# Five mixed chunks of the RWKV receptance kept as parts in DRAM for the second half of the columns

## The chip, the cores and the metric

The kernel runs on one core of one Trainium2 chip. The metric is the time of one execution in device microseconds, as the median of several runs. The core has a matrix engine (TensorE, here PE, with its weight loads shown as PEld), a vector engine (VectorE, DVE), an activation engine (ScalarE, ACT), a general engine (GpSimd, POOL) and a queue engine (SyncE, SP) that issues nearly all DMA transfers of this kernel.

## The reference, cut to what matters

The program is a two-layer causal decoder trunk of 512 positions and 1024 channels in float32. The second layer's mixer is RWKV-7 time mixing. What the change touches is the receptance r:

```
xx = jnp.pad(h, ((0, 0), (1, 0), (0, 0)))[:, :-1] - h
xr, xw, xk, xv, xa, xg = [h + xx * mix[i] for i in range(6)]
r = (xr @ w_r).astype(f32)
...
_, y = lax.scan(rwkv7_step, jnp.zeros((B, H, N, N), f32), seqs)
```

So r is a product of a mixed input (each position blended with the one before it, by one factor per channel) with a 1024 x 1024 matrix. k and v are made in the same way, with other factors. r then enters the recurrence over the positions.

## The kernel before

Channels lie on the partitions, in eight chunks c0 to c7 of 128 channels, with the 512 positions along the free axis. To keep float32 accuracy each operand of a large product is split into two parts, a high part (a cast to the matrix engine's format) and a low part (the value less its high part), and each product is made as three matmuls: high by high, high by low, low by high (`mm3`).

The three projections of RWKV are written by `project`, each in two halves of 512 output columns. A half takes the eight chunks one after the other, with four output banks: for each of c0 to c5 it makes 4 x 3 matmuls, and at its end c6 and c7 are done bank by bank, so that the banks can be evacuated (`evac_r` and others). The weights come as parts from DRAM, where an earlier stage parked them (`L288`), one 512 KB transfer for each chunk and half, into four places that are used in turn.

The mixed chunk that a half needs is made by `mixed`: ACT scales h into a row (`L1361`), DVE adds the scaled neighbour (`L1363`, the blend), ACT casts the row to the high part (`L1372`), and DVE or POOL subtracts for the low part (`L1374`; for r it is DVE for c0 and POOL for the others). For k and v the eight pairs of parts are kept in SBUF for the second half. For r there is no room, and `mixed` is called again in the second half. Here h0 and h1 are the first and the second half of the columns of r, at about 1498 to 1534 us and 1534 to 1575 us of the profiled span.

The counter `n` in `mixed` goes on through all calls: 17 to 24 in h0 of r, 25 to 32 in h1. Where `n % 3` is not 0 the parts of a chunk go to one of two places in `parts_all` (place 0 if `n % 3` is 1, place 1 if it is 2), otherwise to a buffer of the ring `xm`. In h0 these are place 1 for c0, c3 and c6, place 0 for c2 and c5, and xm for c1, c4 and c7; in h1 place 0 for c0, c3 and c6, place 1 for c1, c4 and c7, and xm for c2 and c5.

Beside the halves of r other work is woven in by steps (`weave`): the decay of the second group of heads (`rw_decay`, two products into the banks rq, two evacuations by ACT at `L102`, a running sum on DVE at `L1535` and two exponentials at `L102`), its keys (`rw_keys`), the inverse of the first group (`rw_inverse`, 62 small DVE steps at `L1641` and `L1647`, a 1024-wide ACT copy at `L1656`, writes to and reads from DRAM, and small products), and after h1 the ties and the recurrence, into which the second inverse is woven. The order on PE is pinned as written; the order on the other engines comes from a scheduler that works with modelled times. SP issues its transfers in one order, and a transfer that must wait holds up all behind it.

Of the kernel before, what the change touches and what calls it, by code (L numbers as in the profile page):

```python
# [11 lines left out]
F32 = mybir.dt.float32  # L12
F32R = mybir.dt.float32r
# [6 lines left out]
P = 128  # L20
D = 1024
S = 512
# [27 lines left out]
class Trunk:  # L50
# [1287 lines left out]
    def rwkv(self, gain):  # L1338
        nc, mm = self.nc, self.nc.tensor.matmul
# [12 lines left out]
            )  # L1352

        self.mid = None
        n_mix = [0]

        def mixed(i, c, dep=None):

            n = n_mix[0] = n_mix[0] + 1
            t = self.row("mx", 3) if i == 2 else self.rows[:, n % 2, :]  # L1360
            ins = nc.scalar.activation(t, h[c], AF.Copy, scale=v["mix1"][:, i, c : c + 1])  # L1361
            self.after(ins, dep)
            nc.vector.scalar_tensor_tensor(  # L1363
                out=t[:, 1:], in0=h[c][:, : S - 1], scalar=v["mix"][:, i, c : c + 1], in1=t[:, 1:],
                op0=ALU.mult, op1=ALU.add,
            )
            if i == 0 and n % 3:

                m = self.shaped(self.parts_all[:, (n % 3 - 1) * 2 * S : n % 3 * 2 * S], [2, S])
            else:  # L1370
                m = self.pair("xm", 9, F32R)
            nc.scalar.copy(m[:, 0, :], t)  # L1372
            eng = nc.vector if i == 2 or i == 0 and c == 0 else nc.gpsimd
            eng.tensor_tensor(out=m[:, 1, :], in0=t, in1=m[:, 0, :].bitcast(F32), op=ALU.subtract)  # L1374
            return m[:, 0, :], m[:, 1, :]

        k_t = [None] * NCH
# [28 lines left out]
        def project(half, xm, evac, natural, i_mix=None):  # L1406
# [11 lines left out]
            for k in range(NCH):  # L1418
                if k % 2 == 0:
                    w += self.next_w()  # L1420
                if half == 0 or xm is None:
                    if i_mix == 2:
                        normed(k)
                    xs[k] = mixed(i_mix, k, dep)
                if k < 6:
                    for b in range(4):
                        tile(k, b)
                    if k == 4:
                        self.mid = self.last_mm
                    if k == 5 and i_mix == 2:  # L1430
                        self.after(self.rwkv_tables(), self.last_mm)
                    yield
# [18 lines left out]
        xm = {}  # L1451
# [8 lines left out]
        xm = {}  # L1460
# [507 lines left out]
```

## Time and profile before

| | |
|---|---|
| median of 3 runs | 2130.84 us (2129.04 to 2134.41) |
| the profiled execution's own time | 2133.98 us |
| its span | 2132.3 us |
| mean granted PE clock | 0.985 of full speed |
| PE busy | 2049.5 us, 96% of the span |
| DVE, ACT, POOL busy | 74%, 45%, 6% |
| DMA | 282.42 MB, 132 GB/s over the span |

The profile shows one execution. A row names the line of the kernel, the engine, the operation, and the tiles that it writes and reads. The idle time in brackets is what the engine stood still just before a row, with what ended it. Times within the span are microseconds from its start.

### The profile page before, as it was taken

The numbers are of one execution on the slowest core, as the hardware profiler recorded it, in microseconds if no ns is written. First come the engines' busy times: TensorE is split into PE (matmuls) and PEld (weight loads), VectorE is DVE, ScalarE is ACT, GpSimd is POOL, SyncE is SP. The second block draws the span as 40 slices with busy tenths as digits, with TensorE's granted clock in tenths as the row PEclk, the third lists the DMA queues.
The fourth block names the chain that finished last, engine by engine and source line by source line (L and its number), as shares of the span: only waits on it lengthen the run. The fifth ranks groups of instructions, "written<-read, shape, count | busy, mean of one in ns | idle before, by whom it ended". The sixth has DMA issues, their size and how long they took to land.

```text
span 2132.3 us, 29206 instructions
## 1 busy us (share of the span) xinstructions
PE 2049.5 (96%) x11527; PEld 1642.7 (77%) x11527; DVE 1580.0 (74%) x1985; ACT 960.5 (45%) x1389; POOL 124.1 (6%) x165
## 2 busy tenths in 40 slices
PE   8999999999989999999999999999888999999998
PEld 6788888776877788888878787876666668888887
DVE  7778786467667988797788888556976547887784
ACT  5433444354455544445544444373634425433342
POOL 0000000211000000000000000112332100000000
PEclk9999999999999999999999999999989999999999
DMA  5333332421132567763355664536644232333321
GB/s 169 89 118 101 98 99 72 124 79 51 45 104 62 172 221 240 238 208 127 99 194 187 214 207 158 207 129 207 200 118 107 84 117 86 105 103 119 109 89 40
DMA packets 219297, 282.42 MB, mean 132 GB/s; under 512 B 45395, under 2 KB 135659, under 8 KB 219160
## 3 DMA queue, kind: packets, MB, share of 16 engines
q1 hardware_dynamic: 216520, 278.20, 41.4%
q10 hardware_dynamic: 2640, 2.36, 0.3%
q8 instruction: 91, 1.49, 0.3%
q14 instruction: 46, 0.38, 0.1%
HBM read 227.76 MB, written 54.59 MB: 132 GB/s over the span
## 4 chain that ended last, share of the span: by engine, by line
PE 76%; DVE 12%; DMA 5%; ACT 3%; issue 2%; SPq 1%; POOL 0%; DVEq 0%; ACTq 0%; POOLq 0%
PE fp L120 36%; PE fd L120 17%; PE am L120 6%; PE rm L120 4%; DVE parts L297 2%; PE rq L120 2%; PE wo L120 2%; PE rr L120 2%; PE rl L120 1%; DVE const L1641 1%; DMA wx<-in_rw_wk_dram 1%; DVE const L1647 1%; PE fd L691 1%; ACT parts L296 1%; DVE const L293 1%
## 5 line engine op out<-in xcount | busy, mean ns | idle before, releaser
L120 PE MATMUL fp<-parts,xs 128*128 128x512 f32 x2016 | 493.6, 393 | 11.7 <-DVE parts L297 6.4
L120 PEld LDWEIGHTS fp<-parts,xs 128*128 128x128 f32 x2016 | 378.4, 189 | 95.0 <-DVE parts L297 9.5
L120 PE MATMUL fd<-act,parts 128*128 128x512 f32 x1728 | 409.2, 390 | 2.2 <-DVE acts L332 1.6
L296 ACT CAST parts<-wx 128x1024 fp32r<-128x1024 f32 x224 | 233.9, 1052 | 354.6 <-PE fp L120 167.4
L120 PEld LDWEIGHTS fd<-act,parts 128*128 128x128 f32 x1728 | 323.7, 188 | 72.3 <-DVE acts L332 3.4
L297 DVE TENSOR_TENSOR parts<-wx,parts 128x1024 fp32r<-128x1024 f32 x224 | 272.1, 1220 | 71.3 <-ACT parts L296 71.1
L296 ACT CAST parts<-const 128x1024 fp32r<-128x1024 f32 (+1 forms) x192 | 198.2, 1033 | 267.4 <-PE fp L120 137.0
L120 PE MATMUL fp<-parts,xb 128*128 128x512 f32 x1152 | 291.5, 400 | 6.6 <-ACT wx L668 3.3
L297 DVE TENSOR_TENSOR parts<-const,parts 128x1024 fp32r<-128x1024 f32 (+1 forms) x192 | 230.2, 1200 | 58.1 <-ACT parts L296 57.1
L120 PEld LDWEIGHTS fp<-parts,xb 128*128 128x128 f32 x1152 | 216.2, 191 | 53.5 <-ACT wx L668 3.9
L654 DVE TENSOR_TENSOR wx<-fp,wx 128x1024 f32<-128x1024 f32 x140 | 168.8, 1219 | 24.0 <-PE fp L120 23.8
L712 DVE SCALAR_TENSOR_TENSOR const<-fd,const 128x512 f32<-128x512 f32 x160 | 108.9, 686 | 82.5 <-PE fd L120 82.1
L120 PE MATMUL fp<-parts,xa 128*128 128x512 f32 x576 | 144.6, 400 | 3.0 <-ACT xa L572 2.0
L120 PEld LDWEIGHTS fp<-parts,xa 128*128 128x128 f32 x576 | 110.2, 193 | 27.6 <-ACT xa L572 2.6
L120 PE MATMUL am<-xg,parts 128*128 128x512 f32 x384 | 100.0, 411 | 0.0
L416 POOL TENSOR_TENSOR ssum<-ssum,sq 128x512 f32<-128x512 f32 x14 | 22.9, 1639 | 1180.1 <-ACT sq L415 1179.7
L120 PEld LDWEIGHTS am<-xg,parts 128*128 128x128 f32 x384 | 71.8, 191 | 25.4 <-issue 9.4
L102 ACT ACTIVATE wx<-wx,const 128x512 f32<-128x512 f32 x80 | 53.5, 716 | 47.0 <-DVE wx L654 46.9
L242 ACT CAST acts<-wx 128x1024 fp32r<-128x1024 f32 (+2 forms) x37 | 37.1, 1003 | 53.8 <-DMA wx<-in_rw_wv_dram 14.4
L331 ACT CAST act<-fd 128x512 fp32r<-128x512 f32 x80 | 43.7, 588 | 38.2 <-PE fd L691 38.0
L120 PE MATMUL rm<-xm,parts 128*128 128x512 f32 x252 | 60.8, 394 | 0.0
L243 DVE TENSOR_TENSOR acts<-wx,acts 128x1024 fp32r<-128x1024 f32 (+2 forms) x37 | 43.0, 1163 | 23.8 <-ACT acts L242 23.7
(319 smaller groups left out, 2637.8 us busy)
## 6 DMA issues: line engine op xcount, KB each, us to landing
wx<-in_ffn_w_down_dram SPq DMA_DIRECT2D x72, 512.0 KB
parts<-acts SPq DMA_DIRECT2D x68, 512.0 KB
parts<-parts SPq DMA_DIRECT2D x68, 512.0 KB
wx<-in_ffn_w_gate_dram SPq DMA_DIRECT2D x44, 512.0 KB
wx<-in_ffn_w_up_dram SPq DMA_DIRECT2D x40, 512.0 KB
const<-in_ffn_w_up_dram SPq DMA_DIRECT2D x40, 512.0 KB
const<-in_ffn_w_gate_dram SPq DMA_DIRECT2D x36, 512.0 KB
const<-in_ffn_w_down_dram SPq DMA_DIRECT2D x16, 512.0 KB
```

The source lines that it names most:

```text
L102: ins = nc.scalar.activation(out, in_, func, **kw)
L120: return self.pe(self.nc.tensor.matmul(*args, **kw))
L242: nc.scalar.copy(hi, src)
L243: nc.vector.tensor_tensor(out=lo, in0=src, in1=hi.bitcast(F32), op=ALU.subtract)
L293: self.nc.vector.tensor_tensor(out=out, in0=in0, in1=in1, op=ALU.add)
L296: self.last_cast = self.nc.scalar.copy(hi[:r, :n], raw[:, :n])
L297: self.nc.vector.tensor_tensor(out=lo[:r, :n], in0=raw[:, :n], in1=hi[:r, :n].bitcast(F32), op=ALU.subtract)
L331: self.nc.scalar.copy(hi, t)
L416: nc.gpsimd.tensor_tensor(out=ssum, in0=ssum, in1=sq, op=ALU.add)
L654: add = lambda out, other, ps=ps: nc.vector.tensor_tensor(out=out, in0=ps, in1=other, op=ALU.add)
L691: nc.tensor.transpose(ps[:, b * P : (b + 1) * P], us[n][b][:, f * P : (f + 1) * P], self.ident)
L712: nc.vector.scalar_tensor_tensor(out=self.x[c], in0=ps, scalar=0.5, in1=self.x[c], op0=ALU.mult, op1=ALU.add)
```

## The change

The condition and the placing of the parts are moved into `room`. A chunk of r whose parts went to `parts_all` is stored to a DRAM tile of 512 KB (both parts) right after it is made. Where `mixed` is asked for a chunk that has such a tile, it makes nothing, and loads the parts from DRAM into the place or ring buffer that is its turn. In h0 c0, c2, c3, c5 and c6 are stored, and in h1 they are loaded. The condition of the store stands for both halves.

```diff
-        n_mix = [0]
+        n_mix, kept = [0], {}
...
+            def room():
+                if i == 0 and n % 3:
+
+                    return self.shaped(self.parts_all[:, (n % 3 - 1) * 2 * S : n % 3 * 2 * S], [2, S])
+                return self.pair("xm", 9, F32R)
+
+            if i == 0 and c in kept:
+
+                m = room()
+                self.after(nc.sync.dma_start(m.bitcast(F32), kept[c]), dep)
+                return m[:, 0, :], m[:, 1, :]
             t = self.row("mx", 3) if i == 2 else self.rows[:, n % 2, :]
...
-            if i == 0 and n % 3:
-
-                m = self.shaped(self.parts_all[:, (n % 3 - 1) * 2 * S : n % 3 * 2 * S], [2, S])
-            else:
-                m = self.pair("xm", 9, F32R)
+            m = room()
             nc.scalar.copy(m[:, 0, :], t)
             eng = nc.vector if i == 2 or i == 0 and c == 0 else nc.gpsimd
             eng.tensor_tensor(out=m[:, 1, :], in0=t, in1=m[:, 0, :].bitcast(F32), op=ALU.subtract)
+            if i == 0 and n % 3:
+                kept[c] = self.dram.tile([P, 2, S], F32, name=f"mix{c}")
+                nc.sync.dma_start(kept[c], m.bitcast(F32))
```

The lines below the change stand 11 further down in the changed kernel (`L1600` becomes `L1611`). The order of the instructions on PE stays the same. On ACT, around the change from h0 to h1, the kernel before has from the inverse's 1024-wide copy on (r_10494 to r_10496 are the evacuations r1 to r3 of h0's banks, L1555 a step of the keys, the two L102 rows the exponentials of the fourth decay, the CAST to parts that of c1):

```order
L1656 COPY const_66<-const_66 128x1024
L1600 COPY r_10494<-rm_10280 128x512
L1555 ACTIVATE heads_10336<-pa_10338,const_66 128x512
L1600 COPY r_10495<-rm_10281 128x512
L1372 CAST xm_10584<-const_66 128x512
L1372 CAST parts_67<-const_66 128x512
L1600 COPY r_10496<-rm_10282 128x512
L1562 ACTIVATE heads_10336<-heads_10336 128x8
L102 ACTIVATE heads_10336<-heads_10336 128x512
L102 ACTIVATE us_10337<-heads_10336 128x512
L98 ACT_TABLE_LOAD
```

In the changed kernel ACT has at the same place, from the evacuation r0 (r_10503) on, with r1 to r3 as r_10504 to r_10506:

```order
L1611 COPY r_10503<-rm_10279 128x512
L1667 COPY const_66<-const_66 128x1024
L1566 ACTIVATE heads_10340<-pa_10342,const_66 128x512
L102 ACTIVATE heads_10340<-heads_10340 128x512
L102 ACTIVATE us_10341<-heads_10340 128x512
L98 ACT_TABLE_LOAD
L1380 CAST parts_67<-const_66 128x512
L1611 COPY r_10504<-rm_10280 128x512
L1573 ACTIVATE heads_10340<-heads_10340 128x8
L1611 COPY r_10505<-rm_10281 128x512
L1566 ACTIVATE heads_10340<-pa_10342,const_66 128x512
L1611 COPY r_10506<-rm_10282 128x512
```

The evacuations r1 to r3 moved behind the exponentials, the table load and c1's cast; c2's cast is gone.

On SP the kernel before has, for the time in which h1 begins (parts362 to parts368 are the weights of h1, two chunks each, parts372 weights of a later step, tout0 and uout0 the tiles through which the inverse goes to DRAM and back):

```order
L288 DMA parts_67<-parts372_8060 96x1024
L1655 DMA tout0_10128<-const_66 128x1024
L288 DMA parts_67<-parts364_7674 128x1024
L1662 DMA const_66<-tout0_10128 32x32x32 x2
L288 DMA parts_67<-parts364_7674 128x1024
L1657 DMA uout0_10129<-const_66 128x1024
L288 DMA parts_67<-parts366_7771 128x1024
L1672 DMA us_9526<-uout0_10129 32x32x32 x3
L288 DMA parts_67<-parts366_7771 128x1024
L1672 DMA us_9526<-uout0_10129 32x32x32
L288 DMA parts_67<-parts368_7864 128x1024 x2
```

In the changed kernel the same stretch of SP is (mix1 and mix4 as destinations are stores of c1 and c4 of h1, mix3 as a source the load of c3):

```order
L288 DMA parts_67<-parts372_8060 96x1024
L1666 DMA tout0_10128<-const_66 128x1024
L1668 DMA uout0_10129<-const_66 128x1024
L288 DMA parts_67<-parts364_7674 128x1024 x2
L1673 DMA const_66<-tout0_10128 32x32x32 x2
L1683 DMA us_9526<-uout0_10129 32x32x32
L1385 DMA mix1_10564<-parts_67 128x1024
L1683 DMA us_9526<-uout0_10129 32x32x32 x3
L1370 DMA parts_67<-mix3_10362 128x1024
L288 DMA parts_67<-parts366_7771 128x1024 x2
L1385 DMA mix4_10694<-parts_67 128x1024
L288 DMA parts_67<-parts368_7864 128x1024
```

The store of c1 now stands before three of the four reads of uout0, the load of c3 behind them, and the weights of c4 and c5 (parts366) behind that load.

## Rows read from the trace of the kernel before

**Rows 1.** The page's busy time of PE and its share of the span:

```profile
PE 2049.5 (96%) x11527; PEld 1642.7 (77%) x11527; DVE 1580.0 (74%) x1985; ACT 960.5 (45%) x1389; POOL 124.1 (6%) x165
```

**Rows 2.** Busy time of each engine in stretches of the span (start:end, length, then for each engine its busy us and the number of instructions, the granted PE clock, the share of the DMA engines in use, GB/s):

```profile
1484.00:1488.00 4.00, 4.00 (x18) 3.02 (x18) 0.50 (x3) 0.00 (x0) 0.00 (x0) 1.00 1.02 400
...
1500.00:1512.00 12.00, 11.00 (x48) 7.83 (x46) 11.66 (x20) 4.00 (x10) 6.03 (x6) 1.00 1.02 339
1512.00:1524.00 12.00, 8.06 (x28) 5.45 (x29) 11.52 (x20) 8.78 (x16) 4.29 (x4) 0.80 0.30 103
...
1536.00:1548.00 12.00, 10.19 (x97) 6.78 (x96) 12.00 (x16) 6.61 (x13) 4.00 (x3) 1.00 1.04 257
1548.00:1560.00 12.00, 9.11 (x86) 6.83 (x87) 11.94 (x18) 4.93 (x10) 3.89 (x3) 0.72 0.27 85
```

**Rows 3.** What PE's matmuls waited for in 1498 to 1576 us (us in total, times, longest):

```profile
PE rq L120 <- ACT us L102: 4.2, 2, 3.5
PE rm L120 <- ACT parts L1372: 2.2, 1, 2.2
PE rm L120 <- POOL parts L1374: 2.0, 2, 1.3
...
PE rm L120 <- ACT r L1600: 0.6, 1, 0.6
```

**Rows 4.** PE's timeline (start, us, what, number of matmuls, in brackets the idle time before and what ended it). The row at 1480.28 is in the second half of v; 1520.26 and 1521.84 are in h0, the others in h1:

```profile
1480.28 6.20 PE L120 MATMUL rm<-parts,xm 128*128 128x512 f32 x25 [1.75 <-DMA parts<-parts]
...
1520.26 1.64 PE L120 MATMUL rq<-hids,parts 64*128 64x512 f32 x5 [3.45 <-ACT us L102]
1521.84 5.00 PE L120 MATMUL rm<-parts 128*128 128x512 f32 x12
...
1534.41 2.65 PE L120 MATMUL rm<-parts 128*128 128x512 f32 x9
...
1540.08 2.79 PE L120 MATMUL rm<-parts 128*128 128x512 f32 x11 [0.65 <-POOL parts L1374]
...
1543.22 3.06 PE L120 MATMUL rm<-xm,parts 128*128 128x512 f32 x12
...
1549.56 0.50 PE L120 MATMUL rm<-parts 128*128 128x512 f32 x1 [2.15 <-ACT parts L1372]
1551.40 5.06 PE L120 MATMUL rm<-parts 128*128 128x512 f32 x11 [1.33 <-POOL parts L1374]
...
1557.68 3.04 PE L120 MATMUL rm<-parts 128*128 128x512 f32 x12
```

**Rows 5.** The chain of waits in order of time (start, us, what): the transfer that begins the first inverse, c0's subtraction, the last step of the inverse, c3's blend (DVE counts there from the end of the step before), the subtractions of c4 and c3, PE's last group of h1, and the transfer that begins the second inverse:

```profile
1480.69 6.61 DMA const<-lin
...
1529.57 0.60 DVE parts L1374
...
1531.11 0.19 DVE const L1647
...
1546.89 0.67 DVE const L1363
...
1548.41 2.95 POOL parts L1374 x2
...
1572.11 2.96 PE rm L120 x12
...
1585.20 3.70 DMA const<-lin
```

**Rows 6.** ACT's timeline around the start of h1: the inverse's copy, r1, a key step, r2, c1's cast, r3, the two exponentials, the table load, and the first step of a chunk behind it:

```profile
1532.23 2.13 ACT L1656 COPY const<-const 128x1024 f32<-128x1024 f32 x1
1534.23 0.61 ACT L1600 COPY r<-rm 128x512 f32<-128x512 f32 x1
1534.71 0.85 ACT L1555 ACTIVATE heads<-pa,const 128x512 f32<-128x512 f32 x1
1535.43 0.60 ACT L1600 COPY r<-rm 128x512 f32<-128x512 f32 x1
...
1536.42 0.65 ACT L1372 CAST parts<-const 128x512 fp32r<-128x512 f32 x1
1536.94 0.62 ACT L1600 COPY r<-rm 128x512 f32<-128x512 f32 x1
...
1537.53 0.66 ACT L102 ACTIVATE heads<-heads 128x512 f32<-128x512 f32 x1
1538.05 0.66 ACT L102 ACTIVATE us<-heads 128x512 f32<-128x512 f32 x1
1538.73 1.28 ACT L98 ACT_TABLE_LOAD   x1
1540.02 0.72 ACT L1361 ACTIVATE const<-const 128x512 f32<-128x512 f32 x1
```

**Rows 7.** Timelines of POOL and DVE: a subtraction on POOL, and two steps of the inverse on DVE, one within the POOL row's time and one behind it:

```profile
1493.49 1.62 POOL L1374 TENSOR_TENSOR parts<-const,parts 128x512 fp32r<-128x512 f32 x1 [1.84 <-ACT parts L1372]
...
1493.88 1.41 DVE L1641 TENSOR_TENSOR const<-const 128x156 f32<-128x156 f32 x1
...
1495.68 0.34 DVE L1641 TENSOR_TENSOR const<-const 128x175 f32<-128x175 f32 x1
```

**Rows 8.** SP's timeline: the issue of the first three reads of uout0:

```profile
1542.27 1.53 SPq L1672 DMA_DIRECT2D us<-uout  x3
```

## The prediction

> **What bounds the kernel now.** I read the page's busy shares first: the reader sees TensorE (PE) busy for 96% of the span [rows 1], so nearly everything that a change can win or lose shows as time in which PE stands still or is granted its lower clock. Then the stretches around the change, 1484 to 1560 us, in a table of windows [rows 2]: the clock column is 1.00 except in 1512 to 1524 (0.80) and 1548 to 1560 (0.72), and PE's busy time falls short there and in 1536 to 1548. DVE is full in all rows from 1500 to 1560, and the DMA column says 1.02 in 1500 to 1512, 0.30 after it, and 1.04 in 1536 to 1548.
>
> Next, PE's own waits in these 78 us [rows 3]: 4.2 us for ACT's evacuations of the decay products, 2.2 us for ACT and 2.0 for POOL on the mixed chunks, 0.6 for the evacuation of r. PE's timeline [rows 4] puts them in order. In the first half (h0) PE stands for 3.45 us before the row at 1520.26, and the 12 products behind it take 5.00 us, where 12 take 3.04 in the row at 1557.68. In the second half (h1), whose c0 begins at 1534.41, PE waits 0.6 us for r [rows 3], 0.65 (POOL, c1), 2.15 (ACT, c3) and 1.33 (POOL, c3) [rows 4], and the 11 products of c3 take 5.06 us, against 2.79 for 11 of c1. From 1551.40 on PE does not wait in h1.
>
> Last, the chain of waits [rows 5] shows what is late there: DVE works without a break from the end of the inverse at 1531.30 to 1546.89, where c3's blending step comes up at last; ACT's cast and two POOL subtractions follow, and at 1551.40 PE takes over up to its last product of h1, which starts at 1572.11 in a group of 12. ACT's evacuation, the lin transfers and the second inverse hang on that, so what h1 wins or loses goes through to the end one for one: the recurrence starts from it, and the feed-forward layer behind is PE's own time.
>
> **Removed.** For c0, c2, c3, c5 and c6 of h1 two ACT steps, one DVE blend and one subtraction go (DVE's for c0, POOL's for the rest): 0.72 + 0.65 us of ACT, 0.67 of DVE as the chain counts a blend, and about 1.5 of POOL each (two in 2.95) [rows 5, 6]. None of that counts by itself, since PE is the bound; what counts is that c3 no longer waits behind DVE's queue. Its two waits go, 2.15 + 1.33 us, and so does the low clock behind them, 5.06 - 2.79 = 2.27: together 5.75 us. c4 keeps its own steps, but its blend stands some 20 rows earlier on DVE, inside the inverse, so it isn't late: its cast waits for c1's products only.
>
> **Added on SP.** The condition for a store is the same in both halves, so there are eight stores, not five: c1, c4 and c7 of h1 are written to DRAM too, and nothing loads them. With the five loads that is 13 transfers of 512 KB, 6.8 MB more. A transfer of that size took 3.70 us in a quiet stretch and 6.61 in a full one [rows 5]. c2's and c5's loads go to buffers of their own, long ahead. c0's waits for the last reader of its place, c5 of h0, whose products end by 1526.8 (1521.84 + 5.00) [rows 4]; with 3.70 to 6.61 it lands by 1533.4 at the latest, and PE wants it at 1534. I cost these three at nothing. c3's load stands behind c1's store and the four reads of the inverse, and its place is free when c0 is done, at 1540.1 by the working below: issued at about 1540.9, it lands between 1544.6 and 1547.5, or at 1548.8 with a further 512 KB before it (1.3 us at the 400 GB/s of 1484 to 1488) [rows 2]. PE asks for c3 at 1548.1. So nothing, with 2.0 us as the upper end, if three neighbours and not one come before it. Behind c1's store wait the reads of the inverse: the store waits for POOL's subtraction of c1, some 1.5 us after a cast at 1536.3, so it goes out near 1538.6, and the reads are issued by 1540.5, where in before the first began at 1542.27 [rows 8]. Nothing lost. c6's load waits for c3's products and has some 10 us until PE wants it.
>
> **Moved on ACT.** This is the part that the diff doesn't tell. In before ACT evacuates r1 right behind the 1024-wide copy; now r1, r2 and r3 stand behind that copy, a key step, the two exponentials of the fourth decay, the table load and c1's cast. By the distances of starts [rows 6]: copy 2.00, key step 0.72, exponentials 0.52 and 0.68, table load 1.29, cast 0.52, r1 0.61, together 6.34 us. The copy waits for the inverse, which DVE ended at 1531.30 and now ends 1.3 us sooner (c0's blend 0.67 and subtraction 0.60 gone) [rows 5], at 1530.0; ACT has r0 and one more step ahead of it. I let the copy start at 1531.1, half way between 1530.0 and the 1532.23 of before. Then r1 ends at 1537.4, r2 at 1538.0, r3 at 1539.3, and c0's second group of products waits for r1 from about 1534.8 on, some 2.6 to 3.4 us. c0 ends at 1540.1, the spread product takes 0.4, and c1's 12 products run from 1540.5 to 1543.5, where in before they ended at 1542.8 (the row at 1543.22 less 0.4) [rows 4]: +0.7 us, between -0.4 and +1.8 with the two ends for the copy.
>
> The Trainium skill (ScalarE: Activation LUTs, What ACT_TABLE_LOAD costs) gives a switch of tables 1.28 us for the load and about 1.38 for a drain beside it. The row has 1.28 and the next step starts 0.01 us behind it [rows 6], so this trace shows no drain; by the page r1 would end 1.4 us later and the sum below be -1.8.
>
> **The clock.** A wait of about 3 us lies before c0's second group. In before the stands of 3.45 and of 2.15 + 1.33 us were each followed by the low clock (0.80 and 0.72 over their windows, one of the two levels, 1.2 of 2.4 GHz), at a price of 5.00 - 3.04 = 1.96 and of 2.27 us; the one of 1.75 us at 1480.28 was not: 25 products in 6.20, 0.25 each [rows 2, 4]. I expect the low clock on c1 and c2, at +1.8 (a little under 1.96, since part of it falls on products that wait for r2 and r3 anyway), between 0 and 2.27.
>
> **Sum.** -5.75 + 0.7 + 1.8 = -3.2 us, between -5.75 - 0.4 = -6.2 and -5.75 + 1.8 + 2.27 + 2.0 = +0.3. The profiled execution took 2133.98 us (span 2132.3); it would be 2130.8. The median of before is 2130.84, 3.1 us below that execution; the same 3.2 off it gives 2127.6.
>
> **Rivals.**
> *DVE sets the end (faster).* POOL and DVE hinder each other here: an inverse step of 156 columns took 1.41 us beside a POOL subtraction, one of 175 columns 0.34 alone [rows 7]. Four subtractions fewer give DVE 4 x 1.07, five blends 3.35, c0's subtraction 0.6: 8.2 us. If all of h1 follows DVE, as the chain does up to 1546.89, the time is 2130.84 - 8.2 = 2122.6. Against it: PE's queue is closed from 1551.40 on, and r1 on ACT comes before it. The Trainium skill (GPSIMD Engine Reference, Specifications) says that the two engines share an SBUF interface and contend when DVE reads two SBUF inputs; the rows above agree.
> *The wait only moves (no change).* c3's load lands at 1551 instead of 1548, PE stands about as long as before and the low clock follows it: the 5.75 come back, 2130.8 or up to 1 us on either side. For it: DMA is at 1.04 in 1536 to 1548 [rows 2], and c1's store and c3's load fall into it. Against it: the second load of the c4/c5 weights is pushed behind them.
> *Stores starve h0 (slower).* The stores of c0, c2, c3, c5 and c6 stand on SP before the weight loads of h0, in a stretch with DMA at 1.02 [rows 2], and one waits there for POOL. Each is 1.3 us of transfer; if PE comes to wait for all five, 6.5 us, and for the low clock once, 2.0, the sum is -3.2 + 8.5 = +5.3: 2136.1. It decides once the weights' lead is under 1.3 us. For it: PE waited 1.75 us for weights at 1480.28 [rows 4]. Against it: no such wait leads PE's list after 1498 [rows 3], the DMA column of 1512 to 1524 says 0.30 [rows 2], and one issue of weights per finished chunk leaves a lead of three chunks.
>
> **Chances.** The forecast 0.60, DVE sets the end 0.15, the wait only moves 0.15, stores starve h0 0.10. The three runs of before lie from 2129.04 to 2134.41, and about 0.3% (6.4 us) is what a measurement here can tell from no change: below 2124.4 is faster, above 2137.2 slower. Faster holds most of the first rival and the low edge of the forecast, 0.18; slower half of the last and some of what I haven't thought of, 0.10; the rest, 0.72, is within. The range of 8 in 10 goes from 2121.5 to 2134.5: the sum's ends from the median, 2124.7 and 2131.1, widened by some 3 us on either side for the spread of the runs and the two nearer rivals.
>
> **What would show it.** Right: PE waits about 3 us for ACT r behind c0's first group; no wait for c3, or for DMA, in h1; the low clock on c1 and c2 and not on c3; PE's last group of h1 some 3 us earlier. If PE doesn't wait for r1, the ACT term is wrong; if it waits for a DMA before c3 or c6, the load term; if it waits for weights in h0, the last rival holds. A time under 2122 or over 2135 says that something outside h1 moved.

## The result and the profile after

The changed kernel took 2140.09 us (median of 9 runs, 2135.74 to 2142.79), the kernel before 2134.23 us in the same comparison (9 runs, 2129.04 to 2137.57). The ratio is 1.0027, with a 95% interval from 1.0017 to 1.0036: slower by about 5.9 us, where 3.2 us of gain were forecast, and outside the range.

PE is as full as before [rows 1], at a mean granted clock of 0.982 against 0.985. The page's busy line of the changed kernel:

```profile
PE 2051.9 (96%) x11527; PEld 1647.8 (77%) x11527; DVE 1575.0 (74%) x1979; ACT 953.9 (45%) x1379; POOL 118.2 (6%) x161
```

What PE's matmuls waited for in the halves of r and somewhat beyond, 1498 to 1578 us, which answers to [rows 3]:

```profile
PE rq L120 <- ACT us L102: 3.9, 1, 3.9
PE rm L120 <- ACT r L1611: 2.5, 1, 2.5
PE rm L120 <- DMA parts<-mix: 0.7, 1, 0.7
```

The waits for c1's and c3's parts are gone, and a wait for r has grown from 0.6 to 2.5 us. PE's timeline of h1, which answers to [rows 4], with its first group, c3 and the last group:

```profile
1538.02 0.98 PE L120 MATMUL rm<-parts 128*128 128x512 f32 x3
1541.54 2.74 PE L120 MATMUL rm<-parts 128*128 128x512 f32 x9 [2.54 <-ACT r L1611]
...
1552.88 3.01 PE L120 MATMUL rm<-parts 128*128 128x512 f32 x12 [0.73 <-DMA parts<-mix]
...
1571.28 3.02 PE L120 MATMUL rm<-parts 128*128 128x512 f32 x12
```

The last group of h1 in before:

```profile
1572.04 3.02 PE L120 MATMUL rm<-parts 128*128 128x512 f32 x12
```

h1 begins at 1538.02 and ends at 1571.28 + 3.02 = 1574.30: 36.28 us. In before it took from 1534.41 [rows 4] to 1572.04 + 3.02 = 1575.06: 40.65 us. So h1 gained 4.4 us. ACT's timeline shows why PE waits at its start, as against [rows 6]: r1 (the second copy of r) now stands behind the 1024-wide copy, the key step, the exponentials, the table load and c1's cast.

```profile
1534.69 0.57 ACT L1611 COPY r<-rm 128x512 f32<-128x512 f32 x1
1535.15 2.15 ACT L1667 COPY const<-const 128x1024 f32<-128x1024 f32 x1
...
1539.09 1.28 ACT L98 ACT_TABLE_LOAD   x1
1540.38 0.62 ACT L1380 CAST parts<-const 128x512 fp32r<-128x512 f32 x1
1540.90 0.58 ACT L1611 COPY r<-rm 128x512 f32<-128x512 f32 x1
```

The loss stands behind h1, in a place that the prediction has no step for. In the recurrence the list of PE's waits (1576 to 1712 us) has a new first line; in before no wait for a DMA is in that list:

```profile
PE rr L120 <- DMA const<-vcd: 4.1, 1, 4.1
```

PE's timeline there, first of before, then of after: the four transposes, the products `rr<-const` of the last chunk of the first group of heads, the products of the second inverse, and the next four transposes.

```profile
1633.09 0.66 PE L1729 MATMUL ra<-const 128*128 128x128 f32 x4
1633.67 0.68 PE L120 MATMUL rr<-const 64*64 64x64 f32 x16
1634.28 1.20 PE L120 MATMUL rq<-const,us 32*32 32x32 f32 x64
...
1643.80 0.66 PE L1729 MATMUL ra<-const 128*128 128x128 f32 x4
```

```profile
1631.50 0.66 PE L1740 MATMUL ra<-const 128*128 128x128 f32 x4
1636.27 1.46 PE L120 MATMUL rr<-const 64*64 64x64 f32 x16 [4.11 <-DMA const<-vcd]
1637.65 1.92 PE L120 MATMUL rq<-const,us 32*32 32x32 f32 x64
...
1651.15 1.11 PE L1740 MATMUL ra<-const 128*128 128x128 f32 x4
```

PE came 1.6 us earlier than in before, stood for 4.11 us, and went on with groups that take 1.46 and 1.92 us instead of 0.68 and 1.20. SP's issues tell why, again of before and then of after (start, time of the issuing, what, how many):

```profile
1625.39 0.35 SPq L1655 DMA_DIRECT2D tout<-const  x1
1626.93 1.26 SPq L1707 DMA_DIRECT2D const<-vcd  x2
1628.70 1.30 SPq L1662 DMA_DIRECT2D const<-tout  x2
1630.05 0.60 SPq L1657 DMA_DIRECT2D uout<-const  x1
1633.51 2.28 SPq L1672 DMA_DIRECT2D us<-uout  x4
```

```profile
1623.47 0.34 SPq L1666 DMA_DIRECT2D tout<-const  x1
1626.48 0.94 SPq L1673 DMA_DIRECT2D const<-tout  x2
1627.51 0.67 SPq L1668 DMA_DIRECT2D uout<-const  x1
1630.84 2.79 SPq L1683 DMA_DIRECT2D us<-uout  x4
1633.67 1.26 SPq L1718 DMA_DIRECT2D const<-vcd  x2
```

The two loads of v for that chunk (`const<-vcd`) stood ahead of the second inverse's reads; now they stand behind them. A read of `uout` isn't issued until its write has landed. The Trainium skill (DMA: Bandwidth & Descriptors, Rules for kernel authors) asks for just that: whoever reads what an earlier transfer wrote waits for that transfer's semaphore before issuing. The trace agrees: `uout` was issued at 1627.51, its first read at 1630.84. What it costs here is that SP stands in that wait with two loads behind it that have nothing to do with it. The chain of waits of after shows them on the path:

```profile
1627.51 3.31 DMA uout<-const
1630.84 0.30 SPq L1683
...
1633.67 2.46 DMA const<-vcd
1636.13 0.14 issue
1636.27 1.46 PE rr L120 x16
```

The granted clock of 1632 to 1654 us, in a row of windows of before and one of after (columns as in [rows 2]):

```profile
1632.00:1654.00 22.00, 19.95 (x542) 15.49 (x537) 7.47 (x13) 12.32 (x28) 3.73 (x4) 1.00 0.67 178
```

```profile
1632.00:1654.00 22.00, 17.80 (x410) 15.65 (x410) 3.92 (x6) 8.55 (x19) 2.09 (x2) 0.61 0.59 151
```

From h1's last product to the last `ra` product PE took 130.95 us in before and 137.21 us in after: the 4.4 us won in h1 are lost there, and 1.9 more. The two profiled spans differ by 3.7 us, mainly because two further differences lie outside these stretches: the projections began 3.7 us later in after (1391.64 against 1387.94), and what stands behind the recurrence took 1.8 us less. Between the projections' start and h1 the two differ by 0.1 us.

### The profile page after: what moved, and what is told of

Read it like the earlier page. It is cut to its first block, busy times and chain, and to the rows that moved or that the text cites. A ratio compares the mean times of both kernels' runs of the same rounds, so it can differ in the third digit from the quotient of the medians.

```text
span 2136.0 us, 29213 instructions
## 1 busy us (share of the span) xinstructions
PE 2051.9 (96%) x11527; PEld 1647.8 (77%) x11527; DVE 1575.0 (74%) x1979; ACT 953.9 (45%) x1379; POOL 118.2 (6%) x161
## 4 chain that ended last, share of the span: by engine, by line
PE 77%; DVE 9%; DMA 5%; ACT 3%; issue 3%; SPq 1%; POOL 0%; DVEq 0%; ACTq 0%; POOLq 0%
PE fp L120 37%; PE fd L120 17%; PE am L120 7%; PE rm L120 4%; PE rq L120 2%; DVE parts L297 2%; PE wo L120 2%; PE rr L120 1%; PE rl L120 1%; PE fd L691 1%; DMA wx<-in_rw_wk_dram 1%; ACT parts L296 1%; DVE const L293 1%; DVE wx L293 1%; DMA wx<-in_rw_g_dram 1%
## 5 line engine op out<-in xcount | busy, mean ns | idle before, releaser
L102 ACT ACTIVATE wx<-wx,const 128x512 f32<-128x512 f32 x80 | 53.5, 717 | 45.6 <-DVE wx L654 45.6
```

What stands on the lines that cost most here:

```text
L102: ins = nc.scalar.activation(out, in_, func, **kw)
```

## The experiments

Theory A: the loss is made by the two loads that changed places on SP, and h1's gain is real. Rivals: B, that wait is chance or beside the path; C, the stores cost by their traffic. Later theory D: h1's first wait, for r on ACT, is what is left of the change's price there.

All kernels have the same order on PE. So a profile can be cut at the same products in each of them, by the timelines: h0 (first product of h0 to first of h1), h1 (to the end of its last product), and the recurrence's stretch (to the end of the last `ra` product). Ratios are to the kernel before, each of 5 to 12 runs against 17 to 33 of before (for the changed kernel 9 against 9).

| kernel | h0, us | h1, us | recurrence, us | ratio (95%) |
|---|---|---|---|---|
| before | 36.29 | 40.65 | 130.95 | 1 |
| after | 35.19 | 36.28 | 137.21 | 1.0027 (1.0017 to 1.0036) |
| e0_after_again | 36.54 | 37.94 | 139.45 | 1.0022 (1.0010 to 1.0034) |
| e1_ties_first | 35.35 | 39.42 | 130.65 | 0.9982 (0.9970 to 0.9995) |
| e2_before_ties_last | 35.15 | 43.42 | 138.02 | 1.0035 (1.0024 to 1.0047) |
| e4_five_stores | 35.80 | 40.63 | 130.16 | 0.9984 (0.9973 to 0.9995) |
| e5_r_ahead | 36.57 | 35.19 | 130.00 | 0.9974 (0.9964 to 0.9985) |
| e6_stores_alone | 36.57 | 41.35 | 130.34 | 1.0009 (0.9999 to 1.0018) |
| e7_order_mended | 36.80 | 33.30 | 126.25 | 0.9960 (0.9946 to 0.9973) |
| e8_before_mended | 37.95 | 42.73 | 130.99 | 1.0015 (1.0004 to 1.0026) |
| e9_order_mended_again | 35.87 | 33.88 | 129.73 | 0.9969 (0.9958 to 0.9981) |
| e10_control_c0_free | 35.02 | 37.74 | 130.33 | 0.9987 (0.9976 to 0.9998) |

**The changed kernel again**, without an edit.

> The changed kernel once more, nothing edited. Theory A (the loss is made in the recurrence, by the two const<-vcd loads that now stand behind us<-uout on SP): the row rr<-const 64*64 x16 at about 1636 us again waits about 4.1 us for const<-vcd, a stretch of low clock stands behind it, and the ratio to the kernel before is 1.0017 to 1.0036. Rival B (the gap was chance of that one profile): no such gap here, with the ratio still near 1.0027. Second question: the projections began 3.7 us later in the changed kernel's profile (1391.64 us against 1387.94 us) in code that reads the same in both; if that is scatter, they begin here between 1386 and 1390 us; if it belongs to the changed kernel, at 1391 to 1393 us again.

The wait for `const<-vcd` came back at 4.1 us (4.3 in two waits), the low clock behind it too, and the ratio was 1.0022. So the wait is not chance, as rival B has it. The projections began at 1391.48, as in the first profile; but see the run after the next.

**The two loads back in their place, nothing else.** The tail of the second inverse is written one step later, and its `uout` and `const<-tout` are ordered behind the loads. DVE, ACT, POOL and PE keep their order.

```diff
-        nc.sync.dma_start(du, U)
+        if sg:
+            yield
+        self.after(nc.sync.dma_start(du, U), self.tied_load if sg else None)
...
-            nc.sync.dma_start(t0[lo], src)
+            self.after(nc.sync.dma_start(t0[lo], src), self.tied_load if sg else None)
...
-            self.after(nc.sync.dma_start(sv[own, h], src[:, 4 * sg : 4 * sg + 4, h, :]), self.go)
+            self.tied_load = self.after(nc.sync.dma_start(sv[own, h], src[:, 4 * sg : 4 * sg + 4, h, :]), self.go)
...
-((2, 5, 8, 11, 14, 20, 21, 22, 23), inverse)
+((2, 5, 8, 11, 14, 18, 20, 21, 22, 23), inverse)
```

> The changed kernel with one move on SP: the two const<-vcd loads stand again between tout and const<-tout, as before the change; all else is in the same order on every engine. Theory A: the wait of 4.11 us at 1632 to 1636 us is gone (under 0.5 us), the recurrence runs at the full clock there, and 6.25 us come back: ratio to the kernel before 0.9990 to 1.0005, about 0.0029 under the changed kernel's. Rival B (the gap is beside the path, the loss is made by the heavier DMA traffic of the half before or elsewhere): ratio stays at 1.0017 to 1.0036.

SP issued the loads at 1628.70, before the reads, and the `rr<-const` group on PE began without a wait:

```profile
1628.70 1.25 SPq L1720 DMA_DIRECT2D const<-vcd  x2
1630.04 1.16 SPq L1675 DMA_DIRECT2D const<-tout  x2
```

```profile
1634.85 0.66 PE L1742 MATMUL ra<-const 128*128 128x128 f32 x4
1635.44 0.68 PE L120 MATMUL rr<-const 64*64 64x64 f32 x16
```

The recurrence's stretch was 130.65 us, as in before, and the ratio 0.9982: 0.0040 under the run above, some 8.5 us. That is faster than expected (0.9990 to 1.0005): the loss had been put at 6.25 us, from one profile. On SP the two loads are all that moved. The low clock was not gone, only less (0.84 in 1632 to 1654).

**The kernel before, with the opposite move alone.** Here `ld` is the load of v. ACT, DVE and POOL have the same order as in before, and on SP only the two loads move.

```diff
-                nc.sync.dma_start(dst, src)
+                self.us_loads = self.us_loads + [nc.sync.dma_start(dst, src)] if h or not s else [nc.sync.dma_start(dst, src)]
...
+            for late in self.us_loads if sg == 0 and c == 7 else ():
+                self.after(ld, late)
```

> The kernel before, with the opposite move alone: the two const<-vcd loads behind the four us<-uout on SP, as in the changed kernel; no stores of parts, no loads of parts. Theory A: a wait of 3.5 to 4.5 us for const<-vcd on TensorE in the recurrence, low clock behind it, 4 to 7 us lost: ratio 1.0019 to 1.0033. Rival B: ratio 1.0000 within 0.0008.

No chunk is stored or loaded here, and the wait is there, as long as in after:

```profile
1640.78 0.45 PE L120 MATMUL rr<-const 64*64 64x64 f32 x2 [4.09 <-DMA const<-vcd]
```

The stretch took 138.02 us and the ratio was 1.0035, just above the expected 1.0019 to 1.0033. The move of two small loads makes the loss by itself; theory A holds in both directions. And the projections began at 1391.42 here, in the code of before, where the first profile had 1387.94: the 3.7 us are scatter and no effect of the change.

**Five stores.** The three stores of h1 that nothing loads are left out.

```diff
-            if i == 0 and n % 3:
+            if i == 0 and n % 3 and len(kept) < 5:
```

> The changed kernel without the three stores of the second half that nothing loads (chunks 1, 4 and 7). With them gone the two const<-vcd loads stand by themselves between tout and const<-tout again. Theory A: as e1, ratio 0.9985 to 1.0005; the wait of 0.73 us for c3's load in the second half should fall to 0 to 0.4 us, since one store less stands ahead of it on SP. Rival B: 1.0017 to 1.0036. Rival C (the stores themselves cost, by DMA traffic): e4 is under e1 by 0.0010 or more.

With this condition the scheduler puts the two loads ahead of the reads by itself, and the ratio is that of the run with the order set by hand: 0.9984. ACT and POOL keep the order of after, and DVE differs in one step. So it is the three stores that nothing reads, 70 to 90 us earlier on the queue, that tipped the order; how the scheduler's modelled times came to that is not shown. c3 waited for no load. Besides that the three stores have no price that these intervals (some 0.1% either way) can show.

**The first half's stores alone.** The five stores stay, nothing is loaded, and the loads of v are set ahead.

```diff
-            if i == 0 and c in kept:
+            if i == 0 and c in ():
```

> The five stores of the first half alone: nothing is loaded, all eight chunks are mixed again in the second half, and the const<-vcd loads stand ahead of const<-tout as in the kernel before. It shows what 2.6 MB of stores cost by themselves. Rival C (stores take the DMA queues from the weights and starve the first half): the first half gets longer than its 35 to 36.5 us in the profiles so far, ratio 1.0010 or more. Theory A (the loss came from the order alone): ratio 1.0000 within 0.0010, and the second half 40 to 43.5 us with its waits for c3, as before the change.

1.0009, with an interval from 0.9999 to 1.0018: at the edge of theory A's band, just under rival C's mark, and it doesn't tell no cost from a small loss. Against C: h0 (36.57 us) lies within what kernels without these stores took (35.02 to 37.95), the recurrence (130.34) is as in kernels that gain, and h1 (41.35) as before the change. ACT's and DVE's orders differ from before in about a dozen places each, so this run doesn't give the stores' price alone.

**r ahead on ACT.** To the kernel with five stores, two orders on ACT are added. (A third, the 1024-wide copy behind the evacuation r0, changed nothing: it stood there already.)

```diff
-            nc.scalar.copy(rows[j], ps)
+            self.r_copy = nc.scalar.copy(rows[j], ps)
...
-            ins = nc.scalar.preload_act_table_set(serve[0])
+            ins = self.after(nc.scalar.preload_act_table_set(serve[0]), self.r_copy)
...
-            nc.scalar.copy(m[:, 0, :], t)
+            self.after(nc.scalar.copy(m[:, 0, :], t), self.r_copy if i == 0 else None)
```

> The kernel with five stores, and on ScalarE the table load and c1's cast of the second half set behind the receptances' evacuations r1 to r3 (the 1024 wide copy, the key step and the two exponentials still stand ahead). Theory D (the second half's first wait, 2.54 to 4.77 us for ScalarE's r in the four profiles so far, is what is left of the change's price there): 1.28 us of table load and 0.52 us of cast leave its head, so that wait falls from 3.72 us to about 1.9 us, and the half gets 1.8 us shorter, or 3 us where the low clock behind the wait goes with it; ratio 0.0008 to 0.0014 under the kernel with five stores (0.9984), so 0.9965 to 0.9980. Rival E (the next wait takes its place: c1's cast and subtraction are late by as much): ratio unchanged, 0.9980 to 0.9990.

PE's second group of h1, first with five stores, then here:

```profile
1539.01 4.21 PE L120 MATMUL rm<-parts 128*128 128x512 f32 x9 [3.72 <-ACT r L1611]
```

```profile
1542.76 2.75 PE L121 MATMUL rm<-parts 128*128 128x512 f32 x9 [1.67 <-ACT r L1612]
```

The wait for r was 1.67 us, no low clock followed, h1 took 35.19 us, and the ratio was 0.9974. That is what theory D expects, though h1 is 5.4 us shorter than in the one profile of the kernel with five stores, where 1.8 to 3 were expected. The interval (to 0.9985) reaches that of the kernel with five stores; the profile's rows carry the verdict here, not the times.

**All orders mended.** Beside the above the 1024-wide copy of the first inverse goes behind c1's cast, its `uout` and reads follow it, and the loads of v are set ahead as in e1_ties_first.

```diff
-            nc.scalar.copy(m[:, 0, :], t)
+            self.cast = self.after(nc.scalar.copy(m[:, 0, :], t), self.r_copy if i == 0 else None)
...
+        if not sg:
+            yield
-        (nc.gpsimd.tensor_copy if sg else nc.scalar.copy)(big(U), T.rearrange("p t j -> p j t"))
+        cp = (nc.gpsimd.tensor_copy if sg else nc.scalar.copy)(big(U), T.rearrange("p t j -> p j t"))
+        if not sg:
+            self.after(cp, self.cast)
...
-((2, 3, 4, 5), inverse)
+((1, 2, 3, 4, 5), inverse)
```

> Five stores, the const<-vcd loads ahead of const<-tout, and on ScalarE r1 to r3 and c1's cast ahead of the 1024 wide copy and the table load, whose uout and us<-uout follow later on SP (behind c3's load). Theory D: the wait for r at the start of the second half falls under 0.6 us, c1 waits about 1 us for GpSimd, no low clock follows; the half takes 35 to 37 us against 40.6 us before the change; ratio 0.9955 to 0.9975. Rival E: us lands later by 3 to 4 us, and the inverse's rq<-const,us matmuls at c3 or c4 wait for it; the half stays at 38 to 41 us and the ratio at 0.9980 to 0.9990.

```profile
1538.06 3.06 PE L121 MATMUL rm<-parts 128*128 128x512 f32 x12
1541.04 0.49 PE L121 MATMUL rq<-hids 40*128 40x512 f32 x1
1541.46 3.35 PE L121 MATMUL rm<-parts 128*128 128x512 f32 x12
```

PE goes through c0 and c1 without a wait that the timeline lists; h1 takes 33.30 us, less than theory D's 35 to 37 us, and the ratio is 0.9960. It was run once more:

> The same kernel as e7_order_mended, for a second profile. In the first the stretch from the second half's end to the end of the ra tiles took 126.25 us, against 130.0 to 130.9 us in every other profile without a wait for const<-vcd. If that belongs to the kernel (its half ends without low clock, and us of half 1 is never waited for), it is 125.5 to 127.5 us again; if it is scatter, 129 to 131 us. Ratio 0.9950 to 0.9970 by the first run's interval; the half 33 to 35 us.

h1 33.88 us, ratio 0.9969. The recurrence's stretch was 129.73 us, so the 126.25 us of the first profile were scatter.

**Controls: the same orders without the loads.** The kernel before with the orders of e7_order_mended.

> A control: the kernel before (nothing stored, nothing loaded, all eight chunks mixed again) with the same three orders as the run called e7_order_mended: r1 to r3 and the early casts ahead of the 1024 wide copy on ScalarE, the table load later, const<-vcd ahead of const<-tout. It tells what of that kernel's 0.9960 is the orders alone. If the loads carry the gain (theory F): c3's cast and subtraction are late as in the kernel before (waits of 1.3 to 3.4 us at c3), the second half takes 38 to 42 us and the ratio is 0.9980 to 1.0005. If the orders carry it (rival G): the half takes 33 to 36 us and the ratio is 0.9950 to 0.9970.

```profile
1546.16 5.06 PE L121 MATMUL rm<-parts 128*128 128x512 f32 x11 [7.50 <-DVE parts L1375]
```

This run is no fair control: the order put c0's cast behind r1 to r3 as well, PE waited 7.50 us for c0, and the ratio was 1.0015. With c0 left free:

```diff
-self.r_copy if i == 0 else None
+self.r_copy if i == 0 and c else None
```

> The control again, mended: in e8_before_mended c0's cast was set behind r1 to r3 as well, which the kernels that load c0 don't have to bear (PE waited 7.50 us for c0's subtraction there). Here c0's cast is left free and stands ahead of r0, as in the kernel before; the rest is as in e8_before_mended: nothing stored, nothing loaded, r1 to r3 and c1's cast ahead of the 1024 wide copy, const<-vcd ahead of const<-tout. Theory F (the loads carry the gain): the wait for c3 stays, 2 to 3.5 us, the second half takes 38 to 42 us, ratio 0.9980 to 1.0005. Rival G (the orders carry it): the half takes 33 to 36 us, ratio 0.9950 to 0.9975.

```profile
1546.75 0.49 PE L121 MATMUL rm<-parts 128*128 128x512 f32 x1 [1.86 <-ACT parts L1373]
1548.43 4.33 PE L121 MATMUL rm<-parts 128*128 128x512 f32 x11 [1.19 <-POOL parts L1375]
```

c3 is late as in before, and the ratio is 0.9987. h1 took 37.74 us, a little under the 38 expected. So the orders alone bring some 0.13%, and with the loads it is 0.31 and 0.40%: the loads add 3.8 and 5.8 us. The interval of the first mended run (to 0.9973) lies clear of the control's (from 0.9976), that of the second (to 0.9981) doesn't. The profiles say about 4 us of h1 (33.30 and 33.88 against 37.74), with one profile of the control.

## Why the prediction was wrong

**The step that failed** is "what h1 wins or loses goes through to the end one for one". It was read from PE's and ACT's part of the chain of before, and takes for granted that behind h1 nothing else changes: the recurrence stands at nothing in the sum, and SP's order there was not looked at. There the two loads of v had moved behind a chain of write and read, and PE stood 4.11 us for them. Over the profiles the loss is larger: the recurrence's stretch is 138.2 us in the mean of the three profiles with the loads behind, 129.9 in the mean of the nine with the loads ahead. These 8.3 us and the forecast -3.2 make +5.1, where +5.9 was measured. By the times, e1_ties_first and e2_before_ties_last put the whole move at 8.5 us (1.0022 to 0.9982) and 7.5 us (1.0035; 5.1 to 10.0 by its interval). The passing on itself is sound: in e1_ties_first, with the loads in their old place, the kernel's time fell by about what h1 gains. The prediction's last sign, that a time over 2135 means that something outside h1 moved, held.

Of the 8.3 us some 4.2 are the wait. Some 2.1 lie right behind it: from the `rr<-const` group to the next four transposes (1636.27 to 1651.15 in after, 1633.67 to 1643.80 in before) PE took 14.9 to 15.2 us in the profiles with the wait and 10.1 to 14.6 us, 13.0 in the mean, in those without. That this is the wait's doing is not shown, since the low clock comes there without it too: the windows of 1632 to 1654 show 0.61, 0.62 and 0.69 with the wait, but also 0.69 and 0.77 in e6_stores_alone and e4_five_stores. The last 2.0 us lie for the most part ahead of the wait, where the nine profiles without it differ by 4 us among themselves; their cause is open.

**The gain in h1** held. Forecast 3.2 us; the four profiles with loads and the change's order on ACT (after, e0, e1, e4) took 38.6 us in the mean (36.28 to 40.63), the three that load nothing and whose ACT order wasn't set by hand (before, e2, e6) 41.8 us (40.65 to 43.42): 3.2 us. Its parts hold in the same means: up to the end of c1 +2.7 us (forecast 0.7 + 1.8), behind it -5.9 (forecast -5.75). That the means agree so closely is partly luck, at a spread of 4.4 us over the four profiles and 2.8 over the three. And e1_ties_first, the change without the accident on SP, was 0.18% faster (0.05 to 0.30%), some 3.8 us.

**c3's waits** went, and its low clock with them, as forecast. **ACT's order**: copy to the end of r1 took 1541.48 - 1535.15 = 6.33 us, forecast 6.34; the copy started 0.4 us later against h1 than assumed, and c0's first group took 0.98 us where the prediction lets PE wait from 0.4 us on; the two errors nearly cancel. The table load took 1.28 us and the next step started 0.01 us behind it; the drain of about 1.38 us that the Trainium skill (ScalarE: Activation LUTs, What ACT_TABLE_LOAD costs) gives beside it doesn't show here either. PE's wait was 2.54 us in the first profile, forecast 2.6 to 3.4; the others had 3.66, 4.77 and 3.72. **The low clock behind that wait** (+1.8) did not come in the first profile, and did in the other three: in 1536 to 1548 us the clock was 1.00 there, and 0.86, 0.77 and 0.60 in e0, e1 and e4.

**c3's load** was forecast to land before PE asks. It was issued at 1548.02, 10.0 us into h1 where 6.5 were reckoned, since c1's store and the inverse's reads went out later than thought; PE waited 0.73 us, within the bound of 2.0.

**The rivals.** DVE doesn't set the end: h1's gain is near the sum and far from 8.2 us. The wait only moves: no, PE's 3.5 us before c3 went in all kernels that load c3, and the load was waited for in one profile, 0.73 us. Stores starve h0: no wait for weights leads the list, and h0 took 35.0 to 38.0 us without stores and 35.2 to 36.8 with them. That rival had the sign right and the mechanism wrong: what cost was the order that three of the stores tipped.

**The base.** 2127.6 us also leaned on a median of three runs (2130.84); with 9 to 33 runs before stands at 2134.23 to 2136.9. Of the 12.5 us between forecast and result that is 3.4.

## What to carry to other kernels

When a scheduler orders the queues, a change's effects are to be sought wherever the order differs, also 60 us behind the stage that was edited: compare every queue to the end of the layer, the transfer queue above all, and ask of each small load which waits now stand ahead of it. Loads that depend on nothing recent belong ahead of a write that is read back, by an explicit order. A store that nothing reads showed no price of its own here, but it tipped such an order.

## What was not expected

The place of two small loads on a queue was worth 0.35 to 0.4% of the time, more than the removal of five chunks' blending, casts and subtractions (0.18%). And profiles scatter by several us where the order in the stretch is the same: h1 took 40.65 us in before and 43.42 in e2_before_ties_last, 36.28, 37.94 and 39.42 in after, e0_after_again and e1_ties_first, with waits of other lengths and the low clock behind some of them; a term of 3 us is better read from several profiles than from one.
